# First feed-forward layer of a hybrid decoder step: gate and up as seven block products in place of eight, on an operand normed in front

## The chip, the cores and the metric

The kernel runs on one core of a Trainium2 chip. The metric is the device time of one execution in microseconds. The engines are TensorE (PE, with its weight loads shown as PEld), VectorE (DVE, `V` in the code), ScalarE (ACT, `act`), GpSimd (POOL, `G`) and SyncE (SP), which here only issues transfers.

## What is computed

One step of a decoder layer for 512 prompt tokens and 64 sample tokens (576 in all), of width 1024. The change touches its first part alone, the first half-step feed-forward layer:

```python
D_MODEL, D_FF = 1024, 2816

def rmsnorm(x, w):
    y = x * lax.rsqrt(jnp.mean(x * x, axis=-1, keepdims=True) + RMS_EPS)
    return y * w

def swiglu(x, w_gate, w_up, w_down):
    return (jax.nn.silu(x @ w_gate) * (x @ w_up)) @ w_down

h = x + 0.5 * swiglu(rmsnorm(x, ffn1_norm), ffn1_w_gate, ffn1_w_up, ffn1_w_down)
...
```

After it come the input projection, a state-space scan, attention, the output projection and a second feed-forward layer of the same form. All data are float32.

## The kernel before, in words

Activations lie transposed: a tile holds 128 of the 1024 features on the partitions and the 576 tokens along the row. Tokens are worked in two halves of 288 (`HT`), a row of an accumulator in PSUM. Full float32 precision is made from three matmuls in a faster format (`F32R`): each operand is split into a hi part (a copy rounded to that format, on ACT) and a lo part (the difference, on DVE or POOL), and `mm3` (L204) adds hi x hi, hi x lo and lo x hi for each of the eight blocks of 128 features. So one column tile of 128 outputs and one half of the tokens takes 24 matmuls of 128x128 by 128x288.

`Cols` (L177) loads weight columns, 256 at a time and 512 rows to a transfer (`stage`, L158, four buffers), and `split` (L167) makes hi (L173) and lo (L174) of four 128x128 blocks in one operation of 128x512 each, into four `whi` and four `wlo` buffers. In this layer all lo parts are DVE's (`share[0]` is 0).

`ffn` (L310) runs the layer in two rounds, of 12 and of 10 column tiles. For each column tile f: gate's weights, both halves of the tokens; the eviction from PSUM (L327) multiplies by 0.5 and by the token's norm `nrm.r`; tanh on ACT (L296) and a DVE operation (L297) make silu. Then up's weights, both halves; the eviction (L337) multiplies by the norm, POOL multiplies by silu (L338), ACT makes hi (L339) and POOL lo (L340). When a round's hidden tiles are there, the down product goes over its eight output tiles and adds into `hts` (L349). `done1` (L495) then prepares the next norm's operands.

In front of it (L357 to L394) the input rows are loaded, half of the columns first, then the first gate weights, then the other half; PE transposes them into `hts` (L377, L383); `Norm.add` (L274) multiplies by the norm's weight and splits into hi and lo (L220, L221); and the sums of squares (L391) and the reciprocal root (`rsqrt`, L224) are made beside the first gate products, because the norm itself is needed only at the eviction. Then follow setup pieces that have nothing to do with this layer and run in its idle time: small parameters (L396 to L462), and the running sums of the cached log-forget values (scans on DVE at L474, subtractions on POOL at L485).

The order of the instructions on each engine is set by a planner that simulates the program; `soon()` (L150) raises an operation's priority. Every engine works its own list in order. The pools of PSUM are `acc`, `pv`, `mm` and `tr`, two banks each.

Of the kernel before, what the change touches and what calls it, by code (L numbers as in the profile page):

```python
# [23 lines left out]
P = 128  # L24
OFFSET = 3000
D = 1024
NP = 512
NS = 64
NT = NP + NS
HT = NT // 2  # L30
# [3 lines left out]
NF = DFF // P  # L34
# [59 lines left out]
def build(ctx, tc, A, O):  # L94
    nc = tc.nc
    uid = [0]

    def tl(pool, shape, dt=F32, tag=None, bufs=None):
        uid[0] += 1
        kw = {} if bufs is None else {"bufs": bufs}  # L100
        return pool.tile(shape, dt, tag=tag, name=f"{tag}_{uid[0]}", **kw)

    def pool(name, bufs=1, **kw):
        return tc.tile_pool(name=name, bufs=bufs, **kw)

# [7 lines left out]
    xp = ctx.enter_context(pool("x", bufs=8))  # L113
# [18 lines left out]
    def tr():  # L132
        return bank("tr", 2)

    def sm():
        return bank("mm", 2)
# [6 lines left out]
    def acc():  # L143

        wide[1] += 1
        if wide[0] and wide[1] % 2:
            return pv()[:, :HT]
        return tl(accp, [P, 512], tag="acc")[:, :HT]

    def soon():  # L150

        return tc.high_priority(offset=OFFSET)

    def hs(half):
        return slice(half * HT, (half + 1) * HT)
# [56 lines left out]
    def hilo(hp, view, tagh, tagl, scale=None, n=NT, bufs=None):  # L212

        hi = tl(hp, [P, n], F32R, tag=tagh, bufs=bufs)
        lo = tl(hp, [P, n], F32R, tag=tagl, bufs=bufs)
        if scale is None:
            act(hi, view, AF.Copy)
            V.tensor_tensor(lo, view, hi.bitcast(F32), ALU.subtract)  # L218
        else:
            act(hi, view, AF.Copy, scale=scale)  # L220
            V.scalar_tensor_tensor(lo, view, scale, hi.bitcast(F32), ALU.mult, ALU.subtract)  # L221
        return hi, lo

    def rsqrt(x, n, rp=None, tags=(("rsi", 1), ("rsy", 1), ("rst", 1))):  # L224

        p = x.shape[0]
        i = tl(rp or tp, [p, n], I32, tag=tags[0][0], bufs=tags[0][1])
        V.tensor_scalar(i, x.bitcast(I32), 1, None, ALU.logical_shift_right)
        y = tl(rp or tp, [p, n], tag=tags[1][0], bufs=tags[1][1])
        V.tensor_scalar(y.bitcast(I32), i, -1, 0x5F3759DF, ALU.mult, ALU.add)  # L230
# [37 lines left out]
    class Norm:  # L268


        def __init__(self, wcol, sqp=None, xsp=xp):
# [19 lines left out]
    def silu_half(out, hv, rp):  # L291

        n = hv.shape[-1]
        for o0 in range(0, n, HT):
            th = tl(rp, [P, HT], tag="th", bufs=2)
            act(th, hv[:, o0:o0 + HT], AF.Tanh)  # L296
            V.scalar_tensor_tensor(out[:, o0:o0 + HT], th, 1.0, hv[:, o0:o0 + HT], ALU.add, ALU.mult)  # L297
# [8 lines left out]
    thD = tl(dram, [P, 16, NT], tag="thD")  # L306
    zD = tl(dram, [P, 16, NT], tag="zD")


    def ffn(nrm, cg, wu, wd, hts, done):  # L310

# [41 lines left out]

    with pool("h1", reuse_waits="tile") as hp:
        hts = [tl(hp, [P, NT], tag=f"h{k}") for k in range(8)]
        nrm1 = Norm(0)
        with pool("xin", side="right", reuse_waits="tile") as xi:  # L357
            su = xi
            xin = [tl(xi, [P, D], tag=f"xin{c}") for c in range(5)]
            r1 = tl(su, [8, P], tag="r1")  # L360
# [12 lines left out]
            V.tensor_copy(P1[:, :8], t[:, :8])  # L373
            for k in range(8):
                t = tr()
                for c in range(4):
                    nc.tensor.transpose(t[:, c * P:(c + 1) * P], xin[c][:, k * P:(k + 1) * P], ident)  # L377
                if k % 2:
                    act(hts[k][:, :NP], t, AF.Copy)
                else:  # L380
                    V.tensor_copy(hts[k][:, :NP], t)
                t = sm()
                nc.tensor.transpose(t[:, :NS], xin[4][:NS, k * P:(k + 1) * P], ident[:NS, :NS])  # L383
                V.tensor_copy(hts[k][:, NP:], t[:, :NS])
                nrm1.add(hts[k], squares=False)
            x0 = tl(tp, [P, 5], tag="rsx", bufs=1)
            G.memset(x0, 0.0)
            for c in range(5):
                n = P if c < 4 else NS
                junk = tl(xi, [P, D], tag="junk")  # L390
                act(junk[:n], xin[c][:n], AF.Square, accum_out=x0[:n, c:c + 1])  # L391
# [100 lines left out]

        nrm2 = Norm(8, hp)

        def done1(j):  # L495
            nrm2.add(hts[j])
            nc.scalar.dma_start(out=hD[:, j, :], in_=hts[j])

        ffn(nrm1, cg, A["ffn1_w_up"][0], A["ffn1_w_down"][0], hts, done1)
        nrm2.finish()  # L500

    xs, rbc = nrm2.xs, nrm2.r
# [81 lines left out]
    with pool("att", side="right", reuse_waits="tile") as ap:  # L584
# [155 lines left out]
        class Pair:  # L740
# [384 lines left out]
    with xzs, pool("ssd", side="right", reuse_waits="tile") as wk:  # L1125
# [227 lines left out]
        for j in range(8):  # L1353
            th = tl(xz, [P, NT], tag="cT" if j % 2 else "bT", bufs=2)
            nc.sync.dma_start(out=th, in_=thD[:, 8 + j, :])
            mt = tl(xz, XR, tag="xr", bufs=2)[:, :NT]
            nc.scalar.dma_start(out=mt, in_=mattD[:, j, :])
            V.scalar_tensor_tensor(th, th, 1.0, accs[j], ALU.add, ALU.mult)
            (G if j < 7 else V).tensor_tensor(th, th, mt, ALU.add)
            mhl.append(hilo(xp, th, "xh", "xl"))  # L1360


    hp2 = ctx.enter_context(pool("h2", side="right", reuse_waits="tile"))
# [71 lines left out]
```

## Time and profile before

| | us |
|---|---|
| median of 3 runs | 1915.3 |
| lowest, highest | 1915.18, 1920.16 |
| the profiled execution | 1914.71 |
| its span, first to last instruction | 1912.9 |

The granted TensorE clock of the profiled execution was 0.988 of full speed in the mean. The page gives busy times by engine, forty slices of the span, the chain that ended last, and groups of instructions by line. Every stage has its own limits, so the page's mean is read first and then the stretch that holds the change. A row of the timeline gives start, duration, engine, line and operation; the start to start distance of operations that follow back to back is shorter than their duration, because the end of one overlaps the beginning of the next. The lines themselves stand in the prediction.

### The profile page before, as it was taken

The page shows a single profiled execution, that of the slowest core. Times are in us where ns is not written, and L with a number is a line of the kernel's source. Part 1 is how long each engine was busy: PE and PEld are TensorE (multiplying, and loading weights), DVE is VectorE, ACT ScalarE, POOL GpSimd, SP SyncE. Part 2 cuts the span into 40 slices and gives each one's busy share as a digit, 9 for nine tenths or more (in the row PEclk, how much of TensorE's full clock was granted, in tenths as well). Part 3 has the DMA queues.
Part 4 walks back from the last instruction along what each step waited for, and adds up shares of the span by engine and source line. Part 5 has one row for each costly group of instructions (what it writes and reads, how often), then busy time and mean ns, then how long its engine had stood idle before and what let it go on. Part 6 is the DMA issues. An engine that isn't in the chain of part 4 may idle for free. (4 is left out here: it accounts for less than half of the span.)

```text
span 1912.9 us, 38609 instructions
## 1 busy us (share of the span) xinstructions
PE 1840.0 (96%) x15335; PEld 1731.7 (91%) x15335; DVE 1065.6 (56%) x2204; ACT 748.2 (39%) x1553; POOL 652.2 (34%) x719
## 2 busy tenths in 40 slices
PE   7999999999998999999998988989999999999999
PEld 7999999999896888888997877878889999999998
DVE  4554334445234777775729767888785544334432
ACT  4233223334222555554427455555434333223322
POOL 0433012322322344432227455675744233003310
PEclk9999999999998999999999999999999999999999
DMA  5432223234534787865465545464654332222322
GB/s 152 112 96 80 89 78 89 83 105 111 145 109 129 188 255 223 246 200 148 95 174 153 141 127 142 111 178 124 174 155 136 89 88 77 80 74 81 88 90 71
DMA packets 270841, 243.21 MB, mean 127 GB/s; under 512 B 53276, under 2 KB 243404, under 8 KB 270508
## 3 DMA queue, kind: packets, MB, share of 16 engines
q1 hardware_dynamic: 208208, 169.35, 32.4%
q10 hardware_dynamic: 53092, 36.79, 6.4%
q0 software_dynamic: 9360, 34.61, 5.6%
q8 instruction: 121, 1.98, 0.4%
q14 instruction: 60, 0.49, 0.1%
HBM read 204.97 MB, written 29.03 MB: 122 GB/s over the span
## 5 line engine op out<-in xcount | busy, mean ns | idle before, releaser
L173 ACT ACTIVATE whi<-stage 128x512 fp32r<-128x512 f32 (+2 forms) x474 | 294.6, 622 | 732.4 <-PE acc L209 640.6
L208 PE MATMUL acc<-xh,whi 128*128 128x288 f32 x1856 | 561.7, 303 | 17.8 <-DVE xr L1046 11.5
L209 PE MATMUL acc<-xl,whi 128*128 128x288 f32 x1856 | 552.6, 298 | 0.0
L210 PE MATMUL acc<-xh,wlo 128*128 128x288 f32 x1856 | 552.3, 298 | 0.0
L174 DVE TENSOR_TENSOR wlo<-stage,whi 128x512 fp32r<-128x512 f32 (+1 forms) x373 | 271.9, 729 | 263.9 <-ACT whi L173 243.8
L208 PEld LDWEIGHTS acc<-xh,whi 128*128 128x128 f32 x1856 | 351.0, 189 | 24.8 <-DVE xr L1046 11.5
L209 PEld LDWEIGHTS acc<-xl,whi 128*128 128x128 f32 x1856 | 351.3, 189 | 2.1 <-issue 1.5
L210 PEld LDWEIGHTS acc<-xh,wlo 128*128 128x128 f32 x1856 | 350.7, 189 | 2.0 <-issue 1.3
L338 POOL TENSOR_TENSOR u<-u,s 128x288 f32<-128x288 f32 x88 | 92.1, 1048 | 484.3 <-DVE u L337 427.7
L208 PE MATMUL pv<-xh,whi 128*128 128x288 f32 (+1 forms) x784 | 231.4, 296 | 2.4 <-ACT xh L220 2.2
L209 PE MATMUL pv<-xl,whi 128*128 128x288 f32 (+1 forms) x784 | 231.9, 296 | 0.6 <-DVE xl L218 0.6
L210 PE MATMUL pv<-xh,wlo 128*128 128x288 f32 (+1 forms) x784 | 231.6, 296 | 0.0
L174 POOL TENSOR_TENSOR wlo<-stage,whi 128x512 fp32r<-128x512 f32 (+1 forms) x101 | 138.2, 1368 | 269.6 <-ACT whi L173 255.6
L208 PEld LDWEIGHTS pv<-xh,whi 128*128 128x128 f32 (+1 forms) x784 | 147.3, 188 | 2.9 <-ACT xh L220 2.4
L209 PEld LDWEIGHTS pv<-xl,whi 128*128 128x128 f32 (+1 forms) x784 | 147.2, 188 | 1.2 <-DVE xl L218 0.8
L210 PEld LDWEIGHTS pv<-xh,wlo 128*128 128x128 f32 (+1 forms) x784 | 147.2, 188 | 0.2
L340 POOL TENSOR_TENSOR hl<-u,hh 128x288 fp32r<-128x288 f32 x88 | 77.5, 882 | 81.6 <-ACT hh L339 81.6
L208 PE MATMUL pv<-hh,whi 128*128 128x288 f32 x352 | 104.4, 296 | 0.0
L209 PE MATMUL pv<-hl,whi 128*128 128x288 f32 x352 | 104.3, 296 | 0.0
L208 PE MATMUL acc<-hh,whi 128*128 128x288 f32 x352 | 104.1, 296 | 0.0
L210 PE MATMUL acc<-hh,wlo 128*128 128x288 f32 x352 | 104.1, 296 | 0.0
L209 PE MATMUL acc<-hl,whi 128*128 128x288 f32 x352 | 104.1, 296 | 0.0
(335 smaller groups left out, 3470.0 us busy)
## 6 DMA issues: line engine op xcount, KB each, us to landing
stage<-in_w_in_dram SPq DMA_DIRECT2D x52, 512.0 KB
stage<-in_ffn_w_up_dram SPq DMA_DIRECT2D x44, 512.0 KB
stage<-in_ffn_w_gate_dram SPq DMA_DIRECT2D x43, 512.0 KB
stage<-in_ffn_w_down_dram SPq DMA_DIRECT2D x40, 512.0 KB
pb<-pastD SPq DMA_DIRECT2D x32, 256.0 KB
ab<-cumD SPq DMA_DIRECT2D x32, 256.0 KB
h<-in_state_ssm_dram SPq DMA_DIRECT2D x32, 256.0 KB
out_dram<-h ACTq DMA_DIRECT2D x32, 256.0 KB
```

Source lines behind the costliest of these rows:

```text
L173: act(hi, view, AF.Copy)
L174: e.tensor_tensor(lo, view, hi.bitcast(F32), ALU.subtract)
L208: mm(out, lhsT=hi, rhs=a, start=first and i == 0, stop=False)
L209: mm(out, lhsT=hi, rhs=b, start=False, stop=False)
L210: mm(out, lhsT=lo, rhs=a, start=False, stop=last and i == n - 1)
L338: G.tensor_tensor(u, u, sil[half], ALU.mult)
L340: G.tensor_tensor(hl[:, hs(half)], u, hh[:, hs(half)].bitcast(F32), ALU.subtract)
```

## The change

The two block rows of the features (512 each), the two halves of the tokens and two column tiles make a 2x2 by 2x2 block product. Eight block products become seven (Winograd's form of Strassen), each on sums of blocks. The sums on the side of the activations (`Forms`) are made once and serve all 22 column tiles of gate and of up; those on the side of the weights (`comb`) are made for each pair of column tiles. As the products mix the two halves of the tokens, the norm can't wait for the eviction: it is applied to the input rows before they are transposed. The rounds become 8, 8 and 6 column tiles. The operand buffers of the later layers (`xp`) are allocated only when the forms are free. The second feed-forward layer keeps `ffn`.

```diff
+    class Forms:
+        def __init__(self, fp, tp_, pre):
+            b = [[x[:, :, hs(j)] for j in range(2)] for x in pre]
+            self.f = {}
+            def halves(n, v, e=V):
+                hi = tl(fp, [P, 4, HT], F32R, tag=f"F{n}h")
+                lo = tl(fp, [P, 4, HT], F32R, tag=f"F{n}l")
+                act(hi, v, AF.Copy)
+                e.tensor_tensor(lo, v, hi.bitcast(F32), ALU.subtract)
+                self.f[n] = (hi, lo)
+            def sub(x, y, e=V):
+                t = tl(tp_, [P, 4, HT], tag="Ft", bufs=3)
+                e.tensor_tensor(t, x, y, ALU.subtract)
+                return t
+            halves("11", b[0][0])
+            halves("21", b[1][0])
+            t1 = sub(b[0][1], b[0][0])
+            t2 = sub(b[1][1], t1)
+            halves("t2", t2)
+            halves("t1", t1)
+            halves("t3", sub(b[1][1], b[0][1], G))
+            halves("t4", sub(b[1][0], t2))
+            halves("22", b[1][1], G)
+        def product(self, out, w, n):
+            xh, xl = self.f[n]
+            for i, (hi, lo) in enumerate(w):
+                a, b = xh[:, i, :], xl[:, i, :]
+                mm(out, lhsT=hi, rhs=a, start=i == 0, stop=False)
+                mm(out, lhsT=hi, rhs=b, start=False, stop=False)
+                mm(out, lhsT=lo, rhs=a, start=False, stop=i == 3)
+
+    def winograd(fm, cols, f, rp, scale, take):
+        cols.load(f)
+        (_, s0), (_, s1_) = cols.st
+        a11, a21, a12, a22 = s0[:, :, :P], s0[:, :, P:], s1_[:, :, :P], s1_[:, :, P:]
+        def comb(x, y, op, e=V):
+            t = tl(rp, [P, 4, P], tag="sf", bufs=3)
+            with soon():
+                e.tensor_tensor(t, x, y, op)
+            return t
...
+        def keep(bk, kept=None):
+            t = tl(rp, [P, HT], tag="cp", bufs=5)
+            with soon():
+                if kept is None:
+                    act(t, bk, AF.Copy, scale=scale)
+                elif scale == 1.0:
+                    V.tensor_tensor(t, bk, kept, ALU.add)
+                else:
+                    V.scalar_tensor_tensor(t, bk, scale, kept, ALU.mult, ALU.add)
+            return t
+        def bank_(n):
+            return (lambda: tl(accp, [P, 512], tag="acc"), pv, sm, tr)[n % 4]()[:, :HT]
+        p1 = bank_(0)
+        fm.product(p1, halves(a11), "11")
+        k1 = keep(p1)
+        p2 = bank_(1)
+        fm.product(p2, halves(a12), "21")
+        take(0, 0, p2, k1)
+        s1 = comb(a21, a22, ALU.add)
+        s2 = comb(s1, a11, ALU.subtract)
+        p6 = bank_(2)
+        fm.product(p6, halves(s2), "t2")
+        k2 = keep(p6, k1)
+        p5 = bank_(3)
+        fm.product(p5, halves(s1), "t1")
+        s3 = comb(a11, a21, ALU.subtract, G)
+        p7 = bank_(0)
+        fm.product(p7, halves(s3, G), "t3")
+        k4 = keep(p5, k2)
+        k3 = keep(p7, k2)
+        take(1, 1, p5, k3)
+        p4 = bank_(1)
+        fm.product(p4, halves(a22, G), "t4")
+        take(1, 0, p4, k3)
+        s4 = comb(a12, s2, ALU.subtract)
+        p3 = bank_(2)
+        fm.product(p3, halves(s4), "22")
+        take(0, 1, p3, k4)
```

`halves` in `winograd` is `split` with the engine of the lo part given. `ffn_w` is `ffn` with the loop over pairs of column tiles:

```diff
+            for lo_f, hi_f in rounds:
...
+                for f in range(lo_f, hi_f, 2):
...
+                    def gate(i, half, bk, kept):
+                        g = tl(fp, [P, HT], tag="s", bufs=6)
+                        with soon():
+                            V.scalar_tensor_tensor(g, bk, 0.5, kept, ALU.mult, ALU.add)
+                        silu_half(g, g, fp)
+                        sil[i, half] = g
+                    def up(i, half, bk, kept):
+                        hh, hl = (t[:, hs(half)] for t in pair[i])
+                        u = tl(fp, [P, HT], tag="u", bufs=3)
+                        with soon():
+                            V.tensor_tensor(u, bk, kept, ALU.add)
+                        G.tensor_tensor(u, u, sil[i, half], ALU.mult)
+                        act(hh, u, AF.Copy)
+                        G.tensor_tensor(hl, u, hh.bitcast(F32), ALU.subtract)
+                    winograd(fm, cg, f, fp, 0.5, gate)
+                    winograd(fm, cu, f, fp, 1.0, up)
+                if hi_f == NF:
+                    fm.free()
```

In front, the first gate weights are loaded behind the whole input, and the transposes run twice, on the normed rows for the forms and on the plain rows for `hts`:

```diff
-                if half == 0:
-                    cg = Cols(A["ffn1_w_gate"][0], 0).load(0, (nc.sync, nc.scalar))
+            cg = Cols(A["ffn1_w_gate"][0], 0).load(0, (nc.sync, nc.scalar))
...
-            nrm1.r = spread(rsqrt(x0, 5), 0, tl(tp, [P, NT], tag="rbc", bufs=1))
+            y0 = rsqrt(x0, 5)
+            xn = []
+            for c in range(5):
+                n = P if c < 4 else NS
+                xn.append(tl(xi, [P, D], tag=f"xn{c}"))
+                if c % 2:
+                    V.tensor_scalar(xn[c][:n], xin[c][:n], y0[:n, c:c + 1], None, ALU.mult)
+                else:
+                    act(xn[c][:n], xin[c][:n], AF.Copy, scale=y0[:n, c:c + 1])
...
+            for k in range(8):
+                turned(xn, k, xk[k // 4][:, k % 4, :], P1[:, k:k + 1])
+            fm1 = Forms(fmp, nf, xk)
+            for k in range(8):
+                turned(xin, k, hts[k])
...
+        ffn_w(fm1, cg, A["ffn1_w_up"][0], A["ffn1_w_down"][0], hts, done1, ((0, 8), (8, 16), (16, NF)))
```

`turned` transposes one tile of 128 features by PE and takes it out of PSUM: with the norm's weight, by ACT for odd k and DVE for even k; without one, always by DVE.

More of the change, by code (lines that the diff above doesn't have):

```diff
@@ L112, in build @@
     wp = ctx.enter_context(pool("w"))
-    xp = ctx.enter_context(pool("x", bufs=8))
+    xps = ctx.enter_context(ExitStack())
     tp = ctx.enter_context(pool("tmp", bufs=2))
@@ L268, in build, with __init__ @@
     class Norm:
-        def __init__(self, wcol, sqp=None, xsp=xp):
+        def __init__(self, wcol, sqp=None, xsp=None):
             self.wcol, self.xs, self.n, self.sqp, self.xsp = wcol, [], 0, sqp, xsp
@@ new lines, in winograd, with halves @@
+    def winograd(fm, cols, f, rp, scale, take):
[7 more added lines that the diff above has]
+            return t
+        def halves(v, e=V):
+            hi = tl(wp, [P, 4, P], F32R, tag="whi", bufs=4)
+            lo = tl(wp, [P, 4, P], F32R, tag="wlo", bufs=4)
+            with soon():
+                act(hi, v, AF.Copy)
+                e.tensor_tensor(lo, v, hi.bitcast(F32), ALU.subtract)
+            return [(hi[:, i, :], lo[:, i, :]) for i in range(4)]
+        def keep(bk, kept=None):
[36 more added lines that the diff above has]
+        take(0, 1, p3, k4)
@@ new lines, in ffn_w @@
+    def ffn_w(fm, cg, wu, wd, hts, done, rounds):
+        cu = Cols(wu, 0)
+        with pool("ffnt", bufs=2, reuse_waits="tile") as fp, pool("hid", reuse_waits="tile") as hidp:
+            for lo_f, hi_f in rounds:
+                hid = []
+                n = max(b - a for a, b in rounds)
+                for f in range(lo_f, hi_f, 2):
+                    sil = {}
+                    pair = [(tl(hidp, [P, NT], F32R, tag="hh", bufs=n), tl(hidp, [P, NT], F32R, tag="hl", bufs=n)) for _ in range(2)]
+                    hid += pair
+                    def gate(i, half, bk, kept):
[7 more added lines that the diff above has]
+                        u = tl(fp, [P, HT], tag="u", bufs=3)
+                        with soon():
+                            V.tensor_tensor(u, bk, kept, ALU.add)
[6 more added lines that the diff above has]
+                    fm.free()
+                cd = Cols(wd, 0, k0=lo_f, nk=hi_f - lo_f)
+                for j in range(8):
+                    w = cd.get(j)
+                    for half in range(2):
+                        a = acc()
+                        mm3(a, w, hid, half)
+                        hv = hts[j][:, hs(half)]
+                        with soon():
+                            V.scalar_tensor_tensor(hv, a, 0.5, hv, ALU.mult, ALU.add)
+                    if hi_f == NF:
+                        done(j)
@@ L355, in build @@
         hts = [tl(hp, [P, NT], tag=f"h{k}") for k in range(8)]
-        nrm1 = Norm(0)
-        with pool("xin", side="right", reuse_waits="tile") as xi:
-            su = xi
+        fms = ExitStack()
+        fmp = fms.enter_context(pool("forms", side="right", reuse_waits="tile"))
+        with pool("nf", reuse_waits="tile") as nf, pool("xin", side="right", reuse_waits="tile") as xi:
             xin = [tl(xi, [P, D], tag=f"xin{c}") for c in range(5)]
-            r1 = tl(su, [8, P], tag="r1")
+            r1 = tl(xi, [8, P], tag="r1")
             nc.scalar.dma_start(out=r1, in_=A["ffn1_norm"].rearrange("o (k p) -> (o k) p", p=P))
@@ L373, in build @@
             V.tensor_copy(P1[:, :8], t[:, :8])
[L374 to L385, printed above, removed]
             x0 = tl(tp, [P, 5], tag="rsx", bufs=1)
@@ L493, in build, with free @@
         nrm2 = Norm(8, hp)
+        def free():
+            fms.close()
+            nrm2.xsp = xps.enter_context(pool("x", bufs=8, side="right", reuse_waits="tile"))
+        fm1.free = free
         def done1(j):
@@ L1359, in build @@
             (G if j < 7 else V).tensor_tensor(th, th, mt, ALU.add)
-            mhl.append(hilo(xp, th, "xh", "xl"))
+            mhl.append(hilo(nrm2.xsp, th, "xh", "xl"))
     hp2 = ctx.enter_context(pool("h2", side="right", reuse_waits="tile"))
```

17 lines of the change are left out of this document (16 added, 1 removed).

## The prediction

> **What bounds the kernel now.** I read the page first: busy shares, the slices, the chain.
>
> ```profile
> span 1912.9 us, 38609 instructions
> PE 1840.0 (96%) x15335; PEld 1731.7 (91%) x15335; DVE 1065.6 (56%) x2204; ACT 748.2 (39%) x1553; POOL 652.2 (34%) x719
> ...
> PE   7999999999998999999998988989999999999999
> ...
> DVE  4554334445234777775729767888785544334432
> ...
> POOL 0433012322322344432227455675744233003310
> ...
> PE 35%; DVE 5%; DMA 1%; POOL 1%; issue 1%; ACT 1%; ACTq 0%; SPq 0%; DVEq 0%; POOLq 0%
> ...
> L173 ACT ACTIVATE whi<-stage 128x512 fp32r<-128x512 f32 (+2 forms) x474 | 294.6, 622 | 732.4 <-PE acc L209 640.6
> ```
>
> The first feed-forward layer is the first nine to ten slices, at 48 us each. PE is full there but for the first slice; DVE and POOL are under half. So TensorE bounds the stage. Next I took busy time by stage, cut where the timeline shows the layer's first matmul (15.33), the changes between gate/up and down, and the first matmul of the next layer (450.09).
>
> ```profile
> 15.30:182.90 167.60, 164.42 (x1210) 162.84 (x1211) 87.07 (x179) 60.60 (x118) 51.01 (x64) 0.97 0.36 97
> 182.90:259.30 76.40, 76.40 (x579) 76.40 (x578) 23.95 (x40) 15.64 (x25) 2.68 (x3) 1.00 0.28 83
> 259.30:386.50 127.20, 127.20 (x963) 127.20 (x962) 54.04 (x100) 41.27 (x79) 36.84 (x38) 1.00 0.28 82
> 386.50:450.10 63.60, 63.60 (x483) 63.59 (x482) 26.02 (x46) 22.76 (x39) 11.79 (x10) 1.00 0.41 115
> ```
>
> Columns: stretch, length, then busy time with count of PE, PEld, DVE, ACT, POOL, the granted clock, DMA share, GB/s. By the code the third stretch holds 10 column tiles of 96 matmuls: 127.2/960 = **0.1325 us a matmul**. The first holds 12 tiles, 1152 matmuls, 152.6 us at that pace; it took 167.6, so 15.0 us go in its start. The two down stretches hold 1056 matmuls, 139.9 us at that pace (140.0 seen).
>
> **What is removed.** Per pair of column tiles, gate and up make 2x96 = 192 matmuls now and 2x7x12 = 168 afterwards. Over 11 pairs 264 go: 264 x 0.1325 = **35.0 us of PE**. A pair takes PE 25.4 us now and 22.3 afterwards. The evictions lose their multiplication by the norm. Down keeps its matmuls; three rounds (8, 8, 6 tiles) in place of two add 16 evictions in stages where DVE is a third busy (23.95 of 76.40): nothing. Weight loads keep their number and bytes (DMA share 0.28).
>
> **What a pair adds.** Per call of winograd: seven weight splits (five on V, two on G) where two tiles needed four; four sums of weight blocks (three V, one G), all 128x512 with two SBUF inputs; seven V operations that read a product's PSUM bank (k2, k3, k4 and four takes) where there were four. The silu product (V) and, for up, the multiplication and the lo part (G) stay at four of each per pair. Their prices: the start of one operation to the start of the next where they follow back to back.
>
> ```profile
> 34.35 0.45 DVE L337 TENSOR_TENSOR u<-pv,rbc 128x288 f32<-128x288 f32 x1
> 34.71 0.45 DVE L327 SCALAR_TENSOR_TENSOR g<-acc,rbc 128x288 f32<-128x288 f32 x1
> ...
> 266.44 0.69 DVE L174 TENSOR_TENSOR wlo<-stage,whi 128x512 fp32r<-128x512 f32 x1
> 267.05 0.45 DVE L297 SCALAR_TENSOR_TENSOR s<-th,g 128x288 f32<-128x288 f32 x1
> ```
>
> So 0.36 us for 288 columns and 0.61 for 512 (the durations, 0.45 and 0.69, overlap at their ends). DVE per pair: 16 x 0.61 (ten splits, six sums) + 14 x 0.36 (PSUM) + 4 x 0.36 (silu) = 9.8 + 5.0 + 1.4 = **16.2 us**. ACT: 14 copies at the 0.62 of its row, 10 of 288 columns at under that: below 15 us, no bound.
>
> Now POOL, and what it does to DVE. Two views of the middle of the kernel, first POOL, then DVE at the same moment, then DVE and POOL at 167 to 172 us:
>
> ```profile
> 1119.86 1.30 POOL L1219 TENSOR_TENSOR ab<-ab,cT 128x512 f32<-128x512 f32 x1
> 1121.12 1.29 POOL L1155 TENSOR_TENSOR xg<-xg,zt 128x512 f32<-128x512 f32 x1
> 1122.37 1.28 POOL L1219 TENSOR_TENSOR ab<-ab,cT 128x512 f32<-128x512 f32 x1
> ...
> 1126.52 0.45 POOL L1159 TENSOR_TENSOR ssq<-sq 128x128 f32<-128x128 f32 x1
> ```
>
> ```profile
> 1119.91 7.61 DVE L174 TENSOR_TENSOR wlo<-stage,whi 128x512 fp32r<-128x512 f32 x1
> 1127.44 0.68 DVE L1228 TENSOR_TENSOR xdt<-mm,TT 128x512 f32<-128x512 f32 x1
> ```
>
> ```profile
> 170.46 0.46 DVE L337 TENSOR_TENSOR u<-acc,rbc 128x288 f32<-128x288 f32 x1 [0.39 <-PE acc L210]
> 170.98 0.69 DVE L174 TENSOR_TENSOR wlo<-stage,whi 128x512 fp32r<-128x512 f32 x1
> ```
>
> ```profile
> 167.80 0.80 POOL L338 TENSOR_TENSOR u<-u,s 128x288 f32<-128x288 f32 x1 [6.83 <-DVE u L337]
> 169.76 0.98 POOL L340 TENSOR_TENSOR hl<-u,hh 128x288 fp32r<-128x288 f32 x1 [1.17 <-ACT hh L339]
> 171.00 1.35 POOL L338 TENSOR_TENSOR u<-u,s 128x288 f32<-128x288 f32 x1 [0.26 <-DVE u L337]
> ```
>
> A split on DVE that takes 0.69 us elsewhere took 7.61: it ended 0.55 us after the run of POOL operations did (1126.97). And POOL's 0.80 became 1.35 when a split on DVE had begun 0.02 us before. So a DVE operation with two SBUF inputs and a POOL operation **exclude each other**, the first to start goes on, and a waiting DVE holds up its whole queue, PSUM reads too. A DVE operation with one input in PSUM is free of it: the one at 170.46 began within POOL's 169.76 to 170.74 and took its usual 0.46.
>
> The Trainium skill, page "SBUF — State Buffer", section "Who interferes with whom", says the same: a VectorE instruction with two SBUF inputs contends with a GpSimd one that reads SBUF, and the loser blocks fully. It speaks against this change, which adds only such operations; the 7.61 us agree.
>
> POOL per pair: 6 x 1.25 (four splits, two sums; starts 1.25 apart above) + 8 x 0.78 (just under the 0.80) = **13.7 us**. Of DVE's 16.2 us only the 5.0 on PSUM can lie beside it. So a pair takes at least 16.2 + 13.7 - 5.0 = **24.9 us** and, with nothing alongside, **29.9**; PE wants 22.3. Today the same count is 12.5 (8 splits, 8 PSUM, 4 silu = 9.2 on DVE, 6.2 POOL, less 2.9) to 15.4 against 25.4, which is why nothing of it shows. The bound passes from PE to this pair of engines. Half of the 5.0 alongside gives 27.4; but a DVE operation that waited ends 0.55 after its release and not 0.69, and I guess that seven of twenty wait: less 1.0. I take **26.4 us**. Cover by lookahead is thin: four weight buffers are three products ahead, 3 x 12 x 0.1325 = 4.8 us, and a blocked DVE eats it. Behind a blocked DVE stand the next splits and the takes, and PE waits for both. Up's takes need one of three u buffers, which POOL's lo part sets free: a late POOL stops DVE there too, bounded by the same sums.
>
> **The front.** Now gate begins on the transposed input and its norm comes at the eviction. Afterwards squares, root, scaling, transposes and the sums come first.
>
> ```profile
> 8.27 1.28 ACT L173 ACT_TABLE_LOAD   x1 [8.27 <-DMA xin<-in_x_prompt_dram]
> ...
> 10.18 0.69 DVE L381 COPY h<-tr 128x512 f32<-128x512 f32 x1 [1.03 <-PE tr L377]
> ...
> 11.08 1.06 ACT L391 ACTIVATE junk<-xin 128x1024 f32<-128x1024 f32 x1
> 12.05 0.19 ACT L391 ACTIVATION_READ_ACCUMULATOR junk<-xin 128x1 f32 x1
> ...
> 15.33 0.40 PE L208 MATMUL pv<-xh,whi 128*128 128x288 f32 x1 [2.17 <-ACT xh L220]
> ```
>
> ```profile
> 26.89 0.17 DVE L228 TENSOR_SCALAR rsi<-rsx 128x5 int32<-128x5 int32 x1
> 27.09 0.17 DVE L230 TENSOR_SCALAR rsy<-rsi 128x5 int32<-128x5 int32 x1
> ```
>
> From 9.6 (table loaded): five squares at 1.16 end at 15.4; thirteen small steps at 0.2: 18.0; three scalings on ACT at about 1: 21; four transposed tiles out of PSUM, 0.69 each and as much as 0.2 for the sample's columns, on two engines: 22.8; the first hi copy of 1152 columns, 1.2 by the slope of ACT's rows: the first product at about **24**, 9 us later. Then the seven forms: six lo parts and three differences on DVE, 9 x 1.37 (0.61 scaled) = 12.3, two on POOL at 2.8 = 5.6, which exclude each other; the other evictions, 1.6; half of the call's weight work (the rest runs before 24), PSUM reads and silu, about 6; its three POOL operations, 3.7. Sum 29.2, some 6 us of it alongside: the first gate call ends near **47** (43 to 52). The first gate weights, now behind all of x on both queues, are wanted at 24 and landed before 15: nothing. Setup loads on ACT's queue move back with the front; what they bring is used in setup work alone. The x tiles of the next norm take the forms' place, free before down's last round ends: nothing.
>
> **Sum.** End of the layer = 47 + 10.5 pairs x 26.4 + 139.9 down = 47 + 277.2 + 139.9 = **464.1**, against 450.1: +14.0. Three smaller terms cancel to a few us. At the heads of rounds two and three up to four splits and three sums wait ready, about 5 us each: -10. At each round's end the last u, multiplication, hi and lo run past the matmuls; seven of eight hidden tiles cover 21 x 0.1325 = 2.8 us: 0 to +2 each. And setup work that lay in idle time falls into round one:
>
> ```profile
> L485 POOL TENSOR_TENSOR lg<-pf,st 128x128 f32<-128x128 f32 x16 | 7.1, 481 | 0.0
> L474 DVE TENSOR_TENSOR_SCAN pf<-cst,lg 128x128 f32<-128x128 f32 x16 | 5.9, 438 | 1.1 <-DMA lg<-in_cache_logf_dram,pcol 1.1
> ```
>
> With the evictions of the unnormed input, now all on DVE, some 20 us of DVE and POOL; what the planner leaves for a down stage costs nothing: 0 to +15. The profiled execution took 1914.71 us (span 1912.9, 1.8 us around it), 0.6 under the median of 1915.3: 1914.7 + 14.0, and one for these terms: **1930 us**.
>
> **Rivals.**
> *Faster: the lock is shared well.* Place: the gate/up stages. If all PSUM reads lie beside POOL (24.9) and the heads give back 10: 47 + 261.5 - 10 + 139.9 = 438.4, -11.7, **1903**. If POOL's work drifts into the down stages so far that PE bounds again (22.3): 47 + 234.2 + 139.9 = 421.1, -29, **1886**. It decides below (450.1 - 47 - 139.9)/10.5 = 25.1 us a pair. For: POOL is idle in the down stages (2.68 of 76.40), the heads are ahead. Against: hidden tiles must be whole before down, and buffers allow four splits ahead.
> *No difference*: a pair at 24.6 to 25.6, **1910 to 1921**.
> *Much slower: no overlap*, 29.9, with setup on top: 47 + 314 + 140 + 10 = 511, **1976**. A cold clock would add to it:
>
> ```profile
> 45.00:50.00 5.00, 3.08 (x33) 2.88 (x31) 4.24 (x11) 2.19 (x5) 3.52 (x4) 1.00 0.15 20
> 50.00:55.00 5.00, 5.00 (x29) 4.95 (x28) 2.50 (x5) 1.52 (x3) 3.29 (x4) 0.52 0.16 59
> 55.00:60.00 5.00, 5.00 (x33) 5.00 (x32) 0.92 (x2) 1.06 (x2) 1.95 (x2) 0.80 0.21 36
> ```
>
> After 2 us without PE work and 24x24 transposes the clock fell to 0.52 for 5 us. The gaps I expect are 1 to 3 us, spread; if some cool the clock, each costs 2 to 4 us.
> That the seven products are not made can't be: the code unrolls them.
>
> **How the numbers follow.** Forecast (25.6 to 28.5 a pair, 1921 to 1951) 0.50; faster 0.24 (half of it near 1903, half towards 1886); no difference 0.16; much slower 0.10. The range takes the forecast, no difference and most of the faster case: **1893 to 1960**. A measurement of this kernel can tell about 0.3% from no change: faster 0.24, same 0.16, slower 0.60.
>
> **What would show it.** In the second round: PE below 0.95 busy and waiting for wlo, DVE splits with means well above 0.69, a pair at 26 us. The first product at 24, the first gate call done by 47. Down stages at 0.1325 a matmul. I am wrong if PE stays full in round two (then 1886), or if the time is lost in front and not in the pairs.

## The result and the profile after

The changed kernel took 1963.59 us (median of 4 runs, 1962.37 to 1965.62) against 1917.45 for the kernel before (4 runs, 1915.18 to 1920.16): ratio 1.0241, 95% interval 1.0221 to 1.0261. It is slower, as forecast, but by 46 us where 15 were forecast, and 3.6 us beyond the range. The profiled execution took 1962.37 us, with a span of 1960.6.

The page of the changed kernel, the same lines as before:

```profile
span 1960.6 us, 38555 instructions
PE 1833.5 (94%) x15101; PEld 1709.3 (87%) x15101; DVE 1215.0 (62%) x2389; ACT 795.5 (41%) x1645; POOL 765.2 (39%) x787
...
PE   4599999999999899999998898989999999999999
...
DVE  5597598496424577776646866969676544334432
...
POOL 1275175174322243433224645575844233103220
...
PE 33%; DVE 5%; POOL 2%; issue 2%; DMA 1%; ACT 1%; ACTq 0%; POOLq 0%; DVEq 0%
```

PE has 234 matmul records fewer and yet 6.5 us less busy time only. The hole is in the first two slices, the first 98 us, where PE is at 4 and 5 tenths; DVE is at 5, 5 and then 9. Busy time by stage (stretch, length, then PE, PEld, DVE, ACT, POOL with their counts, granted clock, DMA share, GB/s), cut at the first product, the ends of the first and of the second call of `winograd`, and the changes between gate/up and down:

```profile
15.30:28.90 13.60, 7.94 (x31) 5.31 (x31) 8.25 (x25) 8.17 (x15) 0.00 (x0) 1.00 0.12 37
28.90:77.70 48.80, 32.68 (x162) 26.77 (x161) 33.33 (x52) 13.69 (x20) 11.91 (x6) 0.80 0.17 47
77.70:103.50 25.80, 13.74 (x88) 13.01 (x87) 15.95 (x35) 5.53 (x10) 12.34 (x21) 0.79 0.24 64
103.50:181.90 78.40, 71.38 (x506) 67.61 (x505) 74.29 (x108) 36.30 (x75) 53.27 (x44) 1.00 0.37 94
181.90:232.80 50.90, 50.90 (x386) 50.90 (x385) 19.84 (x35) 11.29 (x19) 5.92 (x6) 1.00 0.32 95
232.80:331.40 98.60, 93.15 (x675) 89.98 (x674) 91.58 (x134) 46.59 (x94) 64.30 (x51) 1.00 0.28 80
331.40:382.30 50.90, 50.90 (x386) 50.90 (x385) 19.79 (x35) 11.24 (x19) 5.88 (x6) 1.00 0.32 95
382.30:454.90 72.60, 69.37 (x506) 67.36 (x505) 67.50 (x100) 34.60 (x70) 46.04 (x37) 1.00 0.25 73
454.90:493.20 38.30, 38.30 (x291) 38.29 (x290) 20.17 (x39) 18.51 (x34) 14.45 (x13) 1.00 0.50 147
```

The layer's last down matmul starts at 493.0 in place of 450.0, 43.0 us later. The three down stretches sum to 140.1 us, as before. Rounds two and three hold seven pairs in 98.6 + 72.6 = 171.2 us, 24.5 a pair and a little under the 25.4 of before: there the change gains. The first two calls, one pair, take from 28.9 to 103.5: 74.6 us for 22.3 us of matmuls. What PE waited for in round one, by the view of the waits (engine, line, what it waited for: us in total, times, longest):

```profile
PE mm L643 <- DVE tot L639: 11.4, 1, 11.4
PE tr L623 <- DMA sc<-in_state_conv_dram: 6.3, 1, 6.3
PE acc L344 <- ACT whi L365: 4.2, 2, 3.8
```

The two longest belong to the setup pieces (the convolution state `sc`, the sums `tot` of the cached log-forget values), not to this layer. In the kernel before, PE waited for the same two pieces as follows:

```profile
PE tr L460 <- DMA sc<-in_state_conv_dram: 1.9, 1, 1.9
PE mm L480 <- DVE tot L476: 0.7, 1, 0.7
```

Two timelines of the changed kernel, DVE and then ACT with its transfer queue:

```profile
68.32 0.17 DVE L612 CAST pf<-pcol 128x8 f32<-128x8 int32 x1 [4.18 <-DMA rq<-in_consts_dram]
```

```profile
62.79 0.36 ACTq L609 DMA_DIRECT2D rq<-in_consts_dram  x1
64.10 0.97 ACTq L618 DMA_DIRECT2D sc<-in_state_conv_dram  x3
```

The loads stand in ACT's list among this layer's hi copies. The first setup load is issued at 43.2 (27.2 in the kernel before) and the loads of `sc` from 64.1 on (41.5 before); in between ACT waited 7.5 us for a sum on DVE and 3.6 us for PE. The setup tiles take the place of the input rows, which PE reads a second time, for `hts`, until 50.1; no row shows a load that waited for that. PE stands at the transposes of `sc` with the next weight product behind them in its list, and DVE stands at `rq` with weight splits behind it. From the start of the last load of `sc` to its first transpose it is 7.3 us here, and 6.9 us in the kernel before. What differs is the work that stands ahead in PE's list meanwhile: 38 matmuls in the kernel before, 8 here.

From here on a number is compared at the **end of the layer** (start of its last down matmul in the trace), because the code behind it is the same in all kernels. The ends are those of the one profiled execution of each kernel, the times are medians.

| kernel | first call ends | end of layer | time, us |
|---|---|---|---|
| before | | 450.0 | 1917.45 |
| changed | 77.5 | 493.0 | 1963.59 |
| e1 setup late | 63.4 | 468.4 | 1940.3 |
| e2 gate/up without POOL | 78.9 | 472.7 | 1929.4 |
| e3 eight products, norm in front | | 470.6 | 1936.7 |
| e4 e1 and e2 together | 64.3 | 448.3 | 1914.4 |
| e5 eight plain tiles first | | 433.6 | 1893.1 |
| e6 four plain tiles first | | 440.8 | 1902.8 |
| e7 e4 and idle POOL work | 69.7 | 502.8 | 1964.2 (1 run) |
| e8 setup at the start | 99.6 | 497.9 | 1964.3 |
| e9 e5, setup at the start | | 473.9 | 1934.6 |
| e10 e5, setup in the down stage | | 454.5 | 1915.8 |
| e11 setup without loads | 67.9 | 478.6 | 1942.3 |

### The profile page after: what moved, and what is told of

It reads as the page before. It is cut to its first block, busy times and chain, and to the rows that moved or that the text cites. A ratio compares the mean times of both kernels' runs of the same rounds, so it can differ in the third digit from the quotient of the medians.

```text
span 1960.6 us, 38555 instructions
## 1 busy us (share of the span) xinstructions
PE 1833.5 (94%) x15101; PEld 1709.3 (87%) x15101; DVE 1215.0 (62%) x2389; ACT 795.5 (41%) x1645; POOL 765.2 (39%) x787
## 5 line engine op out<-in xcount | busy, mean ns | idle before, releaser
L208 PE MATMUL acc<-xh,whi 128*128 128x288 f32 x1504 | 458.4, 305 | 16.1 <-DVE xr L1215 9.7
L209 PE MATMUL acc<-xl,whi 128*128 128x288 f32 x1504 | 449.6, 299 | 0.0
L210 PE MATMUL acc<-xh,wlo 128*128 128x288 f32 x1504 | 449.1, 299 | 0.0
L174 DVE TENSOR_TENSOR wlo<-stage,whi 128x512 fp32r<-128x512 f32 (+1 forms) x285 | 204.1, 717 | 196.9 <-ACT whi L173 186.8
L209 PE MATMUL pv<-xl,whi 128*128 128x288 f32 (+1 forms) x432 | 126.8, 294 | 0.6 <-DVE xl L218 0.6
L210 PE MATMUL pv<-xh,wlo 128*128 128x288 f32 (+1 forms) x432 | 126.9, 294 | 0.0
L208 PE MATMUL pv<-xh,whi 128*128 128x288 f32 (+1 forms) x432 | 126.5, 294 | 0.0
L210 PE MATMUL pv<-hh,wlo 128*128 128x288 f32 x352 | 103.7, 295 | 0.0
L208 PE MATMUL acc<-ygh,whi 128*128 128x288 f32 x256 | 78.9, 308 | 4.6 <-DVE u L1503 4.5
L208 PEld LDWEIGHTS pv<-xh,whi 128*128 128x128 f32 (+1 forms) x432 | 80.0, 185 | 0.2
```

Of the source, the lines that this page charges most:

```text
L174: e.tensor_tensor(lo, view, hi.bitcast(F32), ALU.subtract)
L208: mm(out, lhsT=hi, rhs=a, start=first and i == 0, stop=False)
L209: mm(out, lhsT=hi, rhs=b, start=False, stop=False)
L210: mm(out, lhsT=lo, rhs=a, start=False, stop=last and i == n - 1)
```

## The experiments

**e1: the setup moved behind round one's gate/up.** Theory S: the loss is setup pieces that wait at the head of PE's and DVE's lists. Rival F: it is the chain of forms and the lock, that is, the exclusion of DVE and POOL.

```diff
-        with pool("setup2", side="right", ...) as su:   # and pool("lg"), in front of the layer
+        def setup(): ...                                # the same code
...
                     winograd(fm, cu, f, fp, 1.0, up)
+                if lo_f == 0:
+                    late.append(setup())
```

> The changed kernel, with the setup pieces that do not belong to this layer (small parameters, the running sums of the cached log-forget values) moved from in front of round one to the end of its gate/up stage. All work is kept. Theory S (setup): in round one PE and DVE stand behind setup pieces whose loads start only when the input's buffers come free (PE 6.3 us on sc and 11.4 us on tot, DVE 4.2 us on rq, a clock of 0.8 after them); without them the second call ends near 80 instead of 103.5 and the layer ends near 470 instead of 493: 1938 to 1944 us. Rival F (forms): the sums of the activations and the exclusion of DVE and POOL make the front long and the setup waits only fill the same hole: the second call still ends near 98 and the time is 1955 to 1961.

Measured: 1940.3 us, ratio to before 1.0110 (1.0053 to 1.0167). The second call ended at 75.0 (103.4 in the changed kernel), and the layer 24.5 us earlier. The down stage that now holds most of the setup grew by 4.3 us (55.2 against 50.9). S holds for 24.5 of the 43.0 us. The loads of `sc` were not moved by this: they were issued from 65.9 on, and their transposes ran at 157.7. So it is the place of the pieces in PE's and DVE's lists that costs, not a late load as such.

```profile
29.20:63.50 34.30, 27.28 (x135) 23.02 (x135) 32.89 (x46) 14.18 (x21) 12.23 (x6) 0.85 0.12 34
63.50:153.20 89.70, 82.59 (x591) 78.88 (x590) 80.89 (x126) 40.96 (x84) 59.27 (x47) 1.00 0.31 86
153.20:208.40 55.20, 53.66 (x414) 53.04 (x413) 26.22 (x57) 11.26 (x19) 13.85 (x23) 1.00 0.50 132
```

These stretches of e1 (first call, rest of the round, down) show what is left: in the first call DVE is busy 32.9 of 34.3 us. That part speaks for F, though not for the forms alone: PE is busy 27.3 us in it, 10.6 of them with the transposes of the input, at a granted clock of 0.85.

**e2: gate and up without POOL.** This tells the lock from POOL's usefulness.

```diff
-        s3 = comb(a11, a21, ALU.subtract, G)            # halves(s3, G), halves(a22, G) likewise
+        s3 = comb(a11, a21, ALU.subtract)
...
-                        G.tensor_tensor(u, u, sil[i, half], ALU.mult)   # and the lo part below it
+                        V.tensor_tensor(u, u, sil[i, half], ALU.mult)
```

> The changed kernel with every POOL operation of gate and up given to DVE (one weight sum, two weight splits a call, up's multiplication and lo part); the two operations of the forms on POOL stay. Theory L (lock): DVE then has 22.8 us a pair and nobody to wait for, PE 22.3; a pair of rounds two and three falls from 24.6 to about 23, and the time to about 1950. Rival W (POOL's help is worth more than its lock costs): DVE with 22.8 us a pair in a list worked in order can't keep up, a pair takes 25.5 us or more, and the time is 1970 or over.

Measured: 1929.4 us, 34 us faster than the changed kernel and 20 below the 1950 expected; ratio to before 1.0043 (1.0005 to 1.0081). A pair of round two takes 22.3 us and PE is full. One pair of the changed kernel, then one of e2, by stage:

```profile
279.10:305.00 25.90, 23.66 (x170) 22.50 (x170) 24.04 (x35) 11.66 (x25) 17.78 (x15) 1.00 0.28 82
```

```profile
272.10:294.40 22.30, 22.30 (x170) 22.30 (x169) 21.74 (x46) 12.10 (x24) 0.00 (x0) 1.00 0.33 95
```

DVE has eleven records more in e2 (x46 against x35) and is busy 2.3 us less. Its operations show why; weight splits and sums in the same 52 us (mean ns behind the busy us), changed kernel first:

```profile
L366 DVE TENSOR_TENSOR wlo<-stage,whi 128x512 fp32r<-128x512 f32 x8 | 8.9, 1111 | 0.2
L358 DVE TENSOR_TENSOR sf<-stage,sf 128x512 f32<-128x512 f32 x4 | 6.0, 1488 | 0.1
```

```profile
L366 DVE TENSOR_TENSOR wlo<-stage,whi 128x512 fp32r<-128x512 f32 x9 | 6.0, 681 | 0.1
L358 DVE TENSOR_TENSOR sf<-stage,sf 128x512 f32<-128x512 f32 x3 | 2.0, 680 | 0.0
```

The same operation takes 1111 and 1488 ns beside POOL, 680 without. Theory L holds against W. The end of the layer moved by 20.2 us; the other 14 us lie behind it and are not a gain of this edit as such (see the last section). Some of the 20.2 may be a slow link and not the lock: an operation on POOL takes longer also by itself (1.25 us for 512 columns against 0.61, by the prediction's rows). In round two of the changed kernel PE waited in the end for POOL's lo parts above all:

```profile
PE acc L346 <- POOL wlo L366: 3.1, 2, 1.6
PE pv L346 <- POOL wlo L366: 1.6, 4, 0.6
PE mm L346 <- DVE wlo L366: 0.5, 2, 0.2
```

**e3: the norm in front alone**, with eight products.

```diff
-            fm1 = Forms(fmp, nf, xk)
+            nrm1.xs.append(hilo(fmp, xk[k // 4][:, k % 4, :], "xh", "xl", bufs=8))   # for each k
...
-                            V.scalar_tensor_tensor(g, a, 0.5, nrm.r[:, hs(half)], ALU.mult, ALU.mult)
+                            V.tensor_scalar(g, a, 0.5, None, ALU.mult)               # up: a plain copy
```

> One half of the change alone: the operand normed in front, with the eight block products, rounds and tiles of before (no sums of blocks; evictions without the norm). Theory S: the late start (first product near 25 to 29 instead of 15.3) and the setup loads behind the second set of transposes remain, the chain of forms goes: 1930 to 1942. Rival F: without the forms the front is nearly that of before: 1916 to 1926. Both: the second round takes 12.7 us a column tile as before.

Measured: 1936.7 us, ratio 1.0091 (1.0040 to 1.0142); the layer ends 20.6 us after that of before, first product at 28.0. The second round took 127.2 us, as before. So 20.6 us are lost without any sums of blocks. The later first product makes 12.7 of them. The rest of round one's gate/up is 7.9 us longer, with 5.1 us more PE busy time, the second set of transposes in it. PE waits 6.0 us for `tot` and `sc`, against 17.7 in the changed kernel, although the loads of `sc` come still later here (69.8): 45 matmuls stand between the last of them and the transposes. Late loads alone don't make the changed kernel's price; they do it where little work stands ahead.

**e4: e1 and e2 together.**

> Both edits, setup late and gate/up without POOL. Theories S and L together: 1924 to 1932. F with L: 1942 to 1950. S with W: 1945 or over.

Measured: 1914.4 us, ratio 0.9970 (0.9952 to 0.9987), 10 us below the range that S and L together gave. The layer ends at 448.3: the two gains, 24.5 and 20.2, add up to the 44.7 seen. Within the layer they are two causes, not one.

**e7: POOL work that nobody needs**, added to e4, to see the lock without any dependency.

```diff
+        with soon():
+            idle_pool(2, P)      # G.tensor_tensor(d, d, d, ALU.add) on a tile of its own, 128x512
...
+                        idle_pool(2, 72)     # the same, 128x288, at each of up's takes
```

> The kernel of the last run (setup late, all of gate/up's work on DVE), with POOL operations added that nobody waits for: additions on a tile of its own, as many and of the same sizes as the changed kernel gives to POOL (per pair six of 128x512 and eight of 128x288). Theory L (lock): DVE waits for them, a pair of rounds two and three rises from 22.3 to 24 or more, about as in the changed kernel. Rival (POOL's operations were slow links in the chain from the weights to PE, 1.25 us for 0.6, and no lock is needed): nothing depends on them, a pair stays at 22.3.

Measured: 1964.2 us (one run), 50 more than e4. Of the seven pairs in rounds two and three only the first came above 24 us (28.8); the next two took 23.0 and 23.3, and round three ran as in e4. With nothing in their way these operations run in dense batches, early in each stretch, and not spread as the changed kernel's are. From the second call on, a call takes 17 to 25 us while POOL has a batch (but for the first of round two, 11.4, whose weights stood ready), afterwards 11.1 to 12.3. Two calls of round two, with a batch and just after it:

```profile
260.70:278.10 17.40, 12.48 (x86) 11.32 (x85) 17.40 (x23) 5.81 (x12) 16.13 (x16) 1.00 0.21 62
278.10:290.00 11.90, 11.50 (x87) 11.27 (x86) 11.90 (x26) 5.97 (x12) 0.00 (x0) 1.00 0.27 70
```

And DVE's list within the batch, with POOL's row for it:

```profile
269.61 1.52 DVE L373 TENSOR_TENSOR wlo<-sf,whi 128x512 fp32r<-128x512 f32 x1
271.06 1.15 DVE L365 TENSOR_TENSOR sf<-stage,stage 128x512 f32<-128x512 f32 x1
272.13 0.44 DVE L448 TENSOR_TENSOR u<-pv,cp 128x288 f32<-128x288 f32 x1
```

```profile
261.98 16.02 POOL L353 TENSOR_TENSOR dum<-dum 128x512 f32<-128x512 f32 x14
```

The operations with two SBUF inputs shown here stretch from 0.68 to 1.15 and 1.52 us (others of the batch to 0.78), the one with an input in PSUM keeps its 0.44. Nothing depends on POOL here, so the lock is shown, and no slow link is needed for it. How much of the changed kernel's loss was slow links all the same, no run separates. The Trainium skill, page "SBUF — State Buffer", section "Who interferes with whom", states this rule: a DVE instruction with two SBUF inputs contends with a GpSimd instruction that reads SBUF, one with at most one SBUF input, outside the modes that use two ports, does not. The 1.15, 1.52 and 0.44 agree with it. That the loser waits for the whole of the other operation, as the prediction took it, does not come out of this batch: by the prediction's prices, POOL's 15 operations begun in the 17.4 us and DVE's 15 with two SBUF inputs come to 22.4 us, so some 5 us lay alongside.

**e5 and e6: plain tiles first.** Round one is `ffn` of before; the normed operand and the forms are made on DVE and ACT beside it and its down stage; the rest runs as in e2.

```diff
+            def between():           # called when round one's gate/up is written out
+                for k in range(8):
+                    V.scalar_tensor_tensor(xk[k // 4][:, k % 4, :], hts[k], P1[:, k:k + 1], nrm1.r, ALU.mult, ALU.mult)
+                x1s.close()
+            ffn(nrm1, cg, cu1, A["ffn1_w_down"][0], hts, done1, ((0, 8),), 8, between)
+            fm1 = Forms(...)
...
+        ffn_w(fm1, cg, cu1, A["ffn1_w_down"][0], hts, done1, ((8, 16), (16, NF)))
```

> Seven products from the ninth column tile on: round one (8 tiles) is the plain form of before, with the norm at the eviction and the setup where it was; the normed operand and the seven sums are made on DVE and ACT beside round one and its down stage; the 14 other tiles run as seven products without POOL. If front, setup waits and lock are the whole of the loss, the first stretch is that of before (8 tiles in about 117 us) and the seven pairs take 22.3 in place of 25.4: the layer is 22 us shorter than before's, 1893 to 1900 us. If seven products cost something else (rounds, later stages), 1905 or over.

> The same with four plain tiles and nine pairs, rounds of 4, 6, 6 and 6 tiles. The down stage that hides the sums is only 25 us long and they need 14 us of DVE and 8 of ACT beside 12 of its own: if they hide, 6 us less than with eight tiles, 1887 to 1894; if they don't, 1895 to 1905.

Measured: e5 1893.05 us (6 runs, 1889.7 to 1902.1), ratio 0.9864 (0.9847 to 0.9880): the fastest of this study, faster than both kernels. The time came as expected, but the layer is shorter by 16.4 us and not by 22 in the profiled execution (1901.8): its first stretch took 123.4 us where 117 were expected. e6 1902.8 us, ratio 0.9927 (0.9903 to 0.9950). Round one's down stage and round two's gate/up, e5 first, then e6's down stage:

```profile
137.30:188.30 51.00, 51.00 (x387) 51.00 (x386) 31.50 (x44) 17.63 (x24) 3.72 (x3) 1.00 0.31 94
188.30:278.10 89.80, 89.80 (x678) 89.80 (x677) 87.97 (x182) 47.49 (x93) 0.00 (x0) 1.00 0.30 89
```

```profile
81.30:125.50 44.20, 28.13 (x194) 27.09 (x193) 23.56 (x36) 12.60 (x17) 6.74 (x13) 0.85 0.33 60
```

In e5 the forms cost no time: DVE is busy 31.5 of 51 us and PE is full. In e6 the same work stands in a stage with 25 us of matmuls, and it takes 44.2: the two pairs more in seven products don't pay for that.

**e8, e9, e10: the setup elsewhere.** e8 and e9 (on the changed kernel and on e5) put it at the very start, in the place that the forms or round one's operands take later, with its loads on POOL's queue. e10 puts e5's setup into round one's down stage.

> The changed kernel (POOL in gate and up as it has it) with the same setup work at the very beginning, in the place that the forms take later, its loads on POOL's queue. Nothing of its work goes; its loads no longer wait for the input's buffers. If the 24 us that went with the late setup were waits for loads that began late, they go here too: the waits of PE on sc, tot and of DVE on rq vanish, the layer ends near 470 and the time is 1938 to 1945. If they were work (scans, subtractions, transposes, and their exclusion with POOL), the work now stands in front of the first product or in it: the layer ends at 485 or later, 1953 to 1965.

> Eight plain tiles first, then seven products without POOL, with the setup at the very beginning. The first stretch held 768 matmuls in 123.4 us where 101.8 would do; if the setup's loads are part of that, it falls by 4 to 8 us: 1885 to 1889. If they only get in the way of the input's loads: 1893 or over.

> The same with the setup in the down stage of round one: PE's and DVE's lists are free of it in the first stretch, and it meets the forms in the down stage: 1885 to 1890 if both fit beside the down products, 1893 or over if not.

In all three the hoped-for branch failed, and the times fell into the other one. e8 took 1964.3 us, ratio 1.0272 (1.0243 to 1.0301); e9 1934.6, ratio 1.0114 (1.0088 to 1.0139); e10 1915.8, ratio 1.0006 (0.9987 to 1.0026), 23 us over e5. What ACT waited for, in e8 and then in e10, and ten microseconds of e8:

```profile
ACT F11h L321 <- DMA pastD<-lg: 16.9, 1, 16.9
```

```profile
ACT F11h L321 <- DMA pastD<-lg: 19.1, 1, 19.1
```

```profile
60.00:70.00 10.00, 0.00 (x0) 0.00 (x0) 0.11 (x1) 0.00 (x0) 0.00 (x0) 0.50 0.53 65
```

The forms' tile may be written only when the last store out of `lg`, whose place it takes, is done: no engine works, and the granted clock is 0.50. In e9 the operand `xh` of round one waited 22.0 us in the same way. e8 does not tell waits from work, as it put new waits in the place of the old; it shows that a place in SBUF handed on is a wait for the former owner's transfers.

**e11: the setup in place, its work kept, five of its loads left out.**

```diff
-            for j in range(3):
-                q.dma_start(out=sc[j * B:(j + 1) * B], in_=A["state_conv"][0, :, j, :])
+            G.memset(sc, 0.0)                            # lg, pcol, rq, page likewise
```

> The changed kernel with the setup where it has it, in the input's place, and all its operations on PE, DVE and POOL kept; only five of its loads (sc, pcol twice, rq, lg, page) are left out and their tiles set to zero by POOL, so that the cached log-forget sums and the convolution state come out as those of zeros. If the setup's price in round one is that its loads start when the input's buffers come free and their latency stands in PE's and DVE's lists, the waits on sc, rq and tot shrink to a few us, the layer ends at 468 to 476 in place of 493 and the time is 1936 to 1946. If it is the setup's own work, the layer ends at 485 or later.

Measured: 1942.3 us, ratio 1.0147 (1.0110 to 1.0183); the time is in the range of the first expectation, and the layer ends at 478.6, 14.3 us earlier, between the two. The wait on `sc` is gone and that on `tot` fell from 11.4 to 6.6 us. So of the 24.5 us that e1 wins, some 14 are the latency of loads for which the lists wait; the other 10, by difference, are the setup's own work and its place in the lists.

## Why the prediction was right and wrong

*PE's share, 35.0 us less: right where PE bounds.* e2 and e4 show pairs at 22.3 us with PE full. The three down stretches: 139.9 forecast, 140.1 measured.

*The lock and its price: right, the size in part by luck.* Forecast were 24.9 to 29.9 us a pair, 26.4 taken. The third and fourth pair of round two took 25.9 and 26.3; the first two, with splits and sums ready at the head of the round, 22.4 and 23.9. PE was 0.945 busy there and waited for lo parts, as forecast. But the last 1.0 us of the 26.4 was a guess on how many operations wait, and the 24.9 is no strict bound: in e7's batch a part of the two engines' times lay alongside. That the change "adds only such operations" is not so either; its own sum counts six more reads of PSUM a pair. Seven pairs gave 171.2 us against 7 x 26.4 - 10 = 174.8. "All on PSUM beside POOL" (24.9) was not reached, and the rivals in which PE bounds again were reached only when POOL's work went away.

*The front: wrong in size.* The first product came at 28.9, not 24: PE was full with transposes from 24.0 to 28.9, at 1.34 us a tile, where the forecast priced the evictions on two engines alone. The first call ended at 77.5, not 47, and with most of the setup gone (e1) at 63.4. The forecast listed DVE's and POOL's operations rightly, but counted the copies for `hts` as setup, let some 6 us lie alongside and had no term for PE. In e1 DVE's list ran almost without a pause to the end of the call: copies (5.9 us) and the next call's sums stood ahead of weights that PE was waiting for, and forms waited for POOL's forms. In the changed kernel, DVE first:

```profile
34.43 2.33 DVE L327 TENSOR_TENSOR Ft<-xk,Ft 128x1152 f32<-128x1152 f32 x1
36.68 3.78 DVE L322 TENSOR_TENSOR F21l<-xk,F21h 128x1152 fp32r<-128x1152 f32 x1
```

```profile
32.90 2.64 POOL L327 TENSOR_TENSOR Ft<-xk,xk 128x1152 f32<-128x1152 f32 x1 [32.05 <-ACT xk L548]
35.50 3.75 POOL L322 TENSOR_TENSOR F22l<-xk,F22h 128x1152 fp32r<-128x1152 f32 x1
```

Alone DVE's two take 1.35 each. The front is 16 us of the miss (63.4 against 47); how they divide between DVE's list, PE's 10.6 us of transposes and the lower clock was not separated.

*The setup: the step that failed.* "Setup loads on ACT's queue move back with the front; what they bring is used in setup work alone" priced them at nothing, and the setup's work at 0 to +15, cancelled by the heads of the rounds. Measured 24.5 us (e1), some 14 of it the loads (e11). Setup work alone uses them, but it stands in the lists of PE and DVE among this layer's work, so whoever waits for it stops the layer. The loads moved back by 22.6 us (`sc`, 41.5 to 64.1), the first product by 13.6; and the 7 us until they could be used, which the kernel before covered with 38 matmuls, had 8 ahead of them. Why the lists came out so in the changed kernel and not in e3 is open. A cold clock, which the forecast had beside its slow rival, came too: the granted clock was 0.80 and 0.79 in the first two calls, with gaps of 6.3 and 11.4 us in PE's work, but also 0.85 in e1's first call, which has neither. What it cost was not separated.

*The sum.* Forecast for the end of round one's gate/up: 47 + 3.5 x 26.4 = 139.4; measured 181.9, 42.5 more. Of these, 28.7 go with the setup (153.2 in e1) and 13.8 stay. Rounds two and three with their heads gave 3.6 us back, and the forecast had some 11 us for setup and round ends beside the sum; that leaves the 28 us between 465 and 493. Behind the layer the trace has another 4.6 us, of which the forecast had nothing (see the last section). The test "if the time is lost in front and not in the pairs" was the one that came true.

## What to carry to other kernels

Moving DVE work to POOL was no relief here, where DVE's own operations have two SBUF inputs: count both engines' work as one sum, less what reads PSUM (a cautious sum: e7's batch did 22.4 us of it in 17.4). Here POOL's share went back to DVE and the pair fell from 26 to 22.3 us. When a change moves the start of a stage, list everything else that stands in the same engines' lists, and count the work that stands ahead of it there: its price can be the latency of its loads, which no busy time shows. Work that a new algorithm needs in front is best hidden behind a stretch in the old form, if that stretch is long enough (e5 against e6).

## What the runs showed that was not expected

POOL in a dense queue hardly gives way: in e7's batch its 128x512 additions took 1.29 us in the mean, as without a rival in the prediction's rows (1.28 to 1.30), while DVE's operations of that size with two SBUF inputs took 0.78 to 1.52 us, 1.08 in the mean, against 0.68. POOL was busy 16.1 of 17.4 us meanwhile.

The stretch between this layer and the second feed-forward layer has the same code in all kernels, and yet took 1186.2 us before, 1190.8 in the changed kernel, 1177.8 in e2 and 1193.4 in e1 (last down matmul of the one to the first of the other). PE's busy time there was 1130.6, 1132.8 and 1131.4 in the first three, so it is idle time that differs. The traces show one cause that is e2's alone: its 1645 DVE and 1152 ACT operations of this stretch come in another order than in all the other kernels, and those agree with each other operation for operation. So the 13 us that e2 gains behind the layer go with another order of the planner's and not with POOL's absence; e4, which has the same edit and the usual order, took 1191.9. That the other order is the faster one is likely, but rests on one execution. Among the kernels of the usual order the stretch still runs from 1182.6 (e7) to 1193.4 us. Places in memory are one guess for that; another is that executions differ by themselves, as 13 runs of the kernel before went from 1911.3 to 1927.3 us. Neither was tested. Either puts an uncertainty of some 10 us on any sum for this kernel that is made within one stage, and the 4.6 us above lie within it.
